# The tail of a hybrid attention block: weight parts made in pieces and parked in DRAM, sums on VectorE, products of two groups interleaved

## The chip, the core and the metric

The kernel runs on one core of a Trainium2 chip. The time is the device time of one launch in microseconds (us), the median of several runs. "The profile" is a page on one execution of the program, recorded on the chip; "the trace" is the record behind it, of which other views can be asked. TensorE is called PE there (its weight loads PEld), VectorE DVE, ScalarE ACT, GpSimd POOL and SyncE SP. SyncE computes nothing here: its queue issues the DMAs, in the order of the program.

## The reference

One encoder block over a sequence of 2048 rows of 1024 numbers. Only its end matters here:

```python
proj = h @ w_in                       # h = RMSNorm(x); q, k, v, ga, gb, mg are columns of proj
ya = banded_attention(...) * silu(ga)            # 2048 x 512
yb = sum_g(alpha_g * dilated_group_g(...)) * silu(gb)   # 2048 x 512
br_a, br_b = ya @ w_branch_a, yb @ w_branch_b    # 512 -> 1024 each
gates = sigmoid(mg + b_merge)                    # 2 x 2048 x 1024
merged = gates[0] * br_a + gates[1] * br_b
x = x + merged @ w_out                           # 1024 -> 1024
```

All is float32 and has to be accurate to about that, so each operand of a matmul is split into a high and a low float16 part, and a product is made of three matmuls: high by high, high by low, low by high.

## The kernel before

The kernel has a long part, in which the projections of 14 attention units and the attention itself are interleaved on TensorE (L1070 to L1108), and a **tail** (from L1113), which the change touches. The tail has four stages:

- **Plain gates** (`Std`, L1306): one 128-column chunk of the gate projection for 512 rows, 24 matmuls of 512 columns into one PSUM bank, 5.18 us by the program's plan. ScalarE takes a tanh from the bank, VectorE adds 1 (L1303), SP stores the tile to the DRAM array `mgd` (L1299). Chunk 1 comes first (eight groups), chunk 7 last (eight groups).
- **Gates in seven products** (`GateS`, L1354; `SiluS`, L1380): a 2x2 block product by Strassen's scheme in Winograd's form: seven block products in place of eight, paid for by sums of the operands and of the results. Gate chunks 2 to 6 and the three SiLU chunks 8 to 10 are done so, each in two groups (`SEQ`). A group is 84 matmuls of 512 columns, 18.13 us by plan. Its operands are sums of x (`s_build`, L1162: fourteen sums and differences and four casts for each of 4 chunks and 2 halves, parts on GpSimd and VectorE, into `SH`, `SL`) and sums of the weights (`w_sums` on GpSimd, `s_prep`). A SiLU group loads a tile of the attention output y from the DRAM array `ytd`, multiplies it by SiLU and stores it back.
- **Branches** (`Branch`, L1603): br_a and br_b for 2 x 128 rows, seven products of 24 matmuls of 128 columns. GpSimd multiplies the result by the gates and adds the two branches, and `m_build` makes the sums and float16 parts of `merged` for the last product.
- **Outputs** (`Out`, L1671): seven products of 12 matmuls of 512 columns; VectorE adds each finished bank to x (L1697), and SP stores the result.

The weights of branches and output need sums and float16 parts too: `wb_build` (L1469) makes those of the branches during the last gates and plain gates, `wo_build` (L1566) those of the output weights during the first branches, both from float32 loads, straight into the SBUF tiles that the matmuls read. `y_build` (L1521) does the same for y, its sums on GpSimd.

The seven products of a group use three banks. In `Seven` (L1319) the products have numbers 0 to 6 and the banks 0 to 2:

```python
PROD = (("A11", 0), ("S1", 2), ("A12", 1), ("S2", 0), ("S4", 2), ("S3", 0), ("A22", 0))
```

So product 3 goes on in the bank of product 0, 4 in that of 1, and 5 and 6 again in bank 0. Between two products of one bank its content must be read: by a copy on ScalarE (L1347), a sum on VectorE (L1351), or in `Out` the addition to x (L1697). The order on TensorE is written by hand in `run` (L1420): product 0 of a group, then product 6 of the group before, then products 1 to 5.

```python
def run(g):
    emit(g, 0)
    if pending:
        emit(pending.pop(), 6)
    if g.n == 7:
        for i in range(1, 6):
            emit(g, i)
        pending.append(g)
```

All other work is put on a heap by `at(t, f)` with a planned time t, and `emit` issues what is due between two matmuls. The planned times set only the order of the instructions in each engine's queue; each engine then runs its queue in order and waits for what is missing. Result tiles are `t2` tiles (nine buffers of 128 x 512), raw and summed operands of gates `t3` tiles (eight).

Of the kernel before, what the change touches and what calls it, by code (L numbers as in the profile page):

```python
# [74 lines left out]
Y_MAX = (0.02, 0.445, 0.485)  # L75
X_SQ = (5.098, 1.401, 9.651, 2.051)
# [15 lines left out]
def block_kernel(tc, x, w_units, w_gate, w_mrg, w_out, w_bra, w_brf, gain, qkg, sink, bias_a, bias_b, b_merge, out):  # L92
# [1028 lines left out]
    tp = tl.enter_context(tc.tile_pool(name="tp", bufs=9, reuse_waits="tile"))  # L1121
# [7 lines left out]
    t3p = t3s.enter_context(tc.tile_pool(name="t3p", bufs=8, reuse_waits="tile"))  # L1129
# [3 lines left out]

    def t3():
        return t3p.tile([128, 512], F32, name="t3")

# [25 lines left out]
    def s_build(q, ch):  # L1162
# [10 lines left out]
        def new(k, a, b, op, E=V):  # L1173
            r[k] = t3()
            E.tensor_tensor(r[k][:], a, b, op)  # L1175
# [7 lines left out]
        def lo(j, k):  # L1183
            V.tensor_tensor(SL[q][:, j, ch, :], r[k][:], SH[q][:, j, ch, :], OP.subtract)  # L1184

        return ((0, lambda: new(0, l21, l22, OP.add, G)), (.1, lambda: new(5, l11, l21, OP.subtract, G)),
                (.2, lambda: new(3, h11, h21, OP.subtract, G)),
                (1, lambda: new(1, h21, h22, OP.add)),
                (3, lambda: more(1, r[0][:], OP.add)), (3.1, lambda: hi(0, 1)),
                (4, lambda: more(3, r[5][:], OP.add)), (4.1, lambda: hi(2, 3)),  # L1190
                (5, lambda: new(2, r[1][:], h11, OP.subtract)), (6, lambda: more(2, l11, OP.subtract)),
                (6.1, lambda: hi(1, 2)), (7, lambda: lo(0, 1)), (8, lambda: lo(2, 3)),
                (9, lambda: new(4, h12, r[2][:], OP.subtract)), (10, lambda: more(4, l12, OP.add)),
                (10.1, lambda: hi(3, 4)), (11, lambda: lo(1, 2)), (12, lambda: lo(3, 4)))
# [11 lines left out]
    def w_sums(b11, b12, b21, b22, like, tile):  # L1206

        t = [like(tile()) for _ in range(4)]

        def f1():  # L1210
            G.tensor_tensor(t[0], b12, b11, OP.subtract)

        def f2():
            G.tensor_tensor(t[1], b22, b12, OP.subtract)

        def f3():
            G.tensor_tensor(t[2], t[1], b11, OP.add)

        def f4():
            G.tensor_tensor(t[3], b21, t[2], OP.subtract)  # L1220

        return (b11, t[0], b21, t[2], b22, t[1], t[3]), (f1, f2, f3, f4)
# [4 lines left out]
    def w_ready(dc, b):  # L1227
# [3 lines left out]
        def square(i):  # L1231
            raw = wtiles[u][0]
            if i == 0:
                wtiles[u].append(sm.tile([128, 4], F32, name="wsq"))
            A.activation(t3()[:].rearrange("p (c n) -> p c n", c=2), raw[:, 2 * i:2 * i + 2, :256], AF.Square,
                         accum_out=wtiles[u][1][:, i:i + 1])
# [14 lines left out]
        at(b + 20.5, total)  # L1251
        at(b + 21, power)

    def s_prep(dc, b):
# [4 lines left out]
        def split():  # L1259
# [5 lines left out]
                                lambda t: t[:].rearrange("p (c n) -> p c n", c=4), t3)  # L1265
# [14 lines left out]
        for k, i in enumerate((0, 2, 4, 1, 5, 3, 6)):  # L1280
            at(b + .3 + .9 * k, hi, i)
            at(b + 1.1 + .9 * k, lo, i)
# [18 lines left out]
    def m_gate(dst, src, dc, k, im, t0, d):  # L1301
        at(now[0] + d, lambda: A.activation(dst, src, AF.Tanh, bias=bmh[:, 8 * k + dc:8 * k + dc + 1], scale=im[:]))
        at(now[0] + d + .8, lambda: V.tensor_scalar(dst, dst, 1.0, None, OP.add))  # L1303
# [15 lines left out]
    class Seven:  # L1319
# [25 lines left out]
        def copy(self, j, b):  # L1345
            self.r[j] = t2()
            at(now[0] + .2, lambda: A.activation(self.r[j][:], b[:], AF.Copy))  # L1347

        def sum(self, j, b):
            r = self.r[j]  # L1350
            at(now[0] + .2, lambda: V.tensor_tensor(r[:], b[:], r[:], OP.add))  # L1351
            self.out(j, r, 1.0)
# [27 lines left out]
    class SiluS(GateS):  # L1380
        def __init__(self, g, q):
            super().__init__(8 + g, q)
            self.c0 = 2 + 2 * g

        def silu(self, src, n, t0, d, own):
            im = wtiles[NU + self.dc, "im"]
            c, k = self.c0 + n, 4 * (self.c0 + n) + t0 // 512
            y, th = t2(), t2()
            g = src if own else th
            nc.sync.dma_start(out=y[:], in_=ytd[c, :, t0:t0 + 512])  # L1390
# [28 lines left out]

    def run(g):  # L1420
        emit(g, 0)
        if pending:
            emit(pending.pop(), 6)
        if g.n == 7:
            for i in range(1, 6):
                emit(g, i)
            pending.append(g)

    def flush():
        if pending:  # L1430
            emit(pending.pop(), 6)

    for q in range(2):
        for ch in range(4):
            for d, f in s_build(q, ch):
                at(7.5 * (4 * q + ch) + 12.0 * q + .61 * d, f)
    SEQ = ((2, 0), (3, 0), (2, 1), (3, 1), (8, 0), (8, 1), (9, 0), (9, 1), (10, 0), (10, 1), (4, 0), (4, 1),
           (5, 0), (6, 0), (5, 1), (6, 1))
    first = 41.5
    ready, b = .5, 0.0  # L1440
    for dc, free in ((2, 0.0), (3, 0.0), (8, 3), (9, 4), (10, 6), (4, 8), (5, 10), (6, 12)):
        b = max(first + 18.13 * free + .3 if free else 0.0, ready + 22.0)
        w_ready(dc, ready)
        s_prep(dc, b)
        ready = b + 8.0
    w_ready(7, max(ready, first + 18.13 * 13))
    std_prep(7, first + 18.13 * 15 + .5)
    ym = []
    at(first + 18.13 * 11, lambda: ym.append(y_scale()))
    at(first + 18.13 * 11 + 1.5, lambda: ym.append(norm_sum(ym[0][:], 1)))  # L1450
    at(first + 18.13 * 11 + 2.0, lambda: y_scales(ym[1]))
    wb_raw, WB = {}, [None, None]

    def wb_tiles(k):
        WB[k] = [big(x) for x in "hl"]
# [4 lines left out]
    def wb_load(j):  # L1460
        k, p = divmod(j, 4)
# [355 lines left out]
```

## Time and profile before

| what | value |
| --- | --- |
| median of 3 runs | 2053.19 us (2051.21 to 2054.68) |
| the profiled execution's own time | 2057.84 us |
| its span, first to last instruction | 2056.1 us |
| mean granted TensorE clock | 0.972 |
| busy: PE, PEld | 1923.4, 1462.6 us |
| busy: DVE, ACT, POOL | 1488.5, 1209.0, 821.0 us |
| DMA | 279.79 MB, mean 136 GB/s |

A busy time is the sum over the whole span; it mixes the long part, where TensorE hardly ever pauses, with the tail, where it does. The granted clock is the share of full speed that TensorE was allowed to run at. In a row of groups of instructions a line is one of the kernel file, `fps<-bigh,wh` names what is written and read, and `x256` counts instructions; durations are in ns. A matmul's recorded length is longer than the distance to the next one, since matmuls are pipelined: its pace is read from the starts.

### The profile page before, as it was taken

To read this page: it belongs to the slowest core of one execution; us is meant where nothing else is said; L and a number is where in the kernel's file an instruction comes from. 1 tells how busy PE (TensorE), PEld (TensorE's weight loads), DVE (VectorE), ACT (ScalarE), POOL (GpSimd) and SP (SyncE) were. 2 spreads that over 40 slices of the span, in tenths; PEclk is the share of its full clock that TensorE was granted. 3 is DMA by queue.
4 is the path that set the end of the run, shared out by engine and by line. 5 is a ranking of instruction groups with operands and counts; after the bars stand their busy time and mean duration, and the time that the engine had idled before them with its cause. 6 is when DMAs were issued, how large, how long until landed. Compare 5 with 4: busy or idle time off the path is not lost.

```text
span 2056.1 us, 50959 instructions
## 1 busy us (share of the span) xinstructions
PE 1923.4 (94%) x19278; PEld 1462.6 (71%) x19278; DVE 1488.5 (72%) x3578; ACT 1209.0 (59%) x2917; POOL 821.0 (40%) x1599
## 2 busy tenths in 40 slices
PE   4999999999999999999999999789999985898998
PEld 3568977889998999999998964334444454665664
DVE  5679879867886688668876687965763669666664
ACT  8578768877777677667766663444444544323331
POOL 1033334343543355334533344422121248566552
PEclk9999999999999999999999999899999986999999
DMA  6259998977986698778985682113443253533341
GB/s 233 82 97 197 161 178 145 199 158 137 182 168 133 130 184 154 149 148 135 171 157 105 121 165 80 56 67 122 138 135 119 98 164 98 149 103 119 114 136 55
DMA packets 595446, 279.79 MB, mean 136 GB/s; under 512 B 456704, under 2 KB 550016, under 8 KB 594176
## 3 DMA queue, kind: packets, MB, share of 16 engines
q1 hardware_dynamic: 595200, 276.55, 60.1%
q8 instruction: 150, 2.46, 0.5%
q14 instruction: 96, 0.79, 0.1%
HBM read 115.75 MB, written 50.59 MB: 81 GB/s over the span
## 4 chain that ended last, share of the span: by engine, by line
PE 74%; DVE 12%; DMA 5%; issue 3%; ACT 3%; POOL 2%; SPq 1%; DVEq 0%; POOLq 0%; ACTq 0%
PE pj L625 40%; PE fps L1367 11%; PE fps L1616 6%; PE fps L1690 5%; PE s L775 4%; PE pv L824 4%; PE pj L287 3%; DMA pt<-p 2%; DVE mf L1663 2%; DVE t L1178 1%; DVE bigl L1184 1%; DVE t L1175 1%; PE fps L287 1%; DMA kq<-spl 1%; DVE wl L1275 1%
## 5 line engine op out<-in xcount | busy, mean ns | idle before, releaser
L625 PE MATMUL pj<-wl,XH 128*128 128x128 f16 (+2 forms) x2816 | 716.0, 268 | 0.0
L625 PE MATMUL pj<-wh,XL 128*128 128x128 f16 (+2 forms) x2816 | 712.3, 269 | 0.0
L625 PE MATMUL pj<-wh,XH 128*128 128x128 f16 (+2 forms) x2816 | 709.5, 268 | 0.0
L625 PEld LDWEIGHTS <-XH 128*128 128x128 f16 x5632 | 575.4, 112 | 54.6
L625 PEld LDWEIGHTS <-XL 128*128 128x128 f16 x2816 | 316.0, 112 | 24.1
L790 DVE CUSTOM_DVE_ANT_0 pr<-s,b,ubuf 128x256 f32<-128x256 f32 (+3 forms) x512 | 219.2, 465 | 70.2 <-PE s L775 66.9
L807 DVE SCALAR_TENSOR_TENSOR p<-pr,p 128x512 f16<-128x512 f32 (+2 forms) x256 | 194.9, 761 | 66.0 <-ACT p L803 62.0
L692 POOL TENSOR_TENSOR rw<-rw,g 128x128 f32<-128x128 f32 (+1 forms) x224 | 136.2, 628 | 210.9 <-DVE rw L685 191.4
L1616 PE MATMUL fps<-y,bigh 128*128 128x128 f16 x1792 | 166.3, 228 | 35.4 <-ACT t L1347 24.2
L707 POOL COPY spl<-spl 128x256 f16<-128x256 f16 (+1 forms) x224 | 87.8, 421 | 258.7 <-DVE spl L702 258.7
L1367 PEld LDWEIGHTS <-wh 128*128 128x128 f16 x896 | 89.3, 100 | 135.7 <-issue 36.0
L643 ACT ACTIVATE rw<-pj 128x256 f32<-128x256 f32 (+1 forms) x224 | 87.4, 390 | 167.1 <-PE pj L625 166.6
L1616 PEld LDWEIGHTS <-bigh 128*128 128x128 f16 x1792 | 147.7, 103 | 42.1 <-issue 38.1
L1690 PE MATMUL fps<-WOh,mf 128*128 128x512 f16 x448 | 147.1, 401 | 25.5 <-DVE xr L1697 25.5
L803 ACT ACTIVATE p<-pr 128x512 f16<-128x512 f32 (+2 forms) x256 | 157.7, 616 | 15.5 <-DMA pt<-p 10.9
L1616 PE MATMUL fps<-y,bigl 128*128 128x128 f16 x896 | 163.6, 228 | 0.0
L775 PE MATMUL s<-kq 128*128 128x128 f16 (+1 forms) x1856 | 148.4, 218 | 5.8 <-DMA kq<-spl 4.9
L775 PEld LDWEIGHTS <-kq 128*128 128x128 f16 x2016 | 131.0, 98 | 22.2 <-issue 6.7
L1690 PEld LDWEIGHTS <-mf 128*128 128x128 f16 x672 | 67.6, 102 | 110.3 <-issue 43.3
L1347 ACT ACTIVATE t<-fps 128x512 f32<-128x512 f32 x96 | 56.7, 591 | 144.4 <-PE fps L1616 111.2
L824 PE MATMUL pv<-vt,pt 128*128 128x65 f16 (+1 forms) x2784 | 131.6, 193 | 8.9 <-DMA pt<-p 8.9
L824 PEld LDWEIGHTS <-pt 128*128 128x128 f16 x3024 | 119.5, 97 | 24.6 <-DMA pt<-p 11.4
(245 smaller groups left out, 4162.1 us busy)
## 6 DMA issues: line engine op xcount, KB each, us to landing
wraw<-in_w_units_dram SPq DMA_DIRECT2D x56, 384.0 KB, 4.7
g<-mgd SPq DMA_DIRECT2D x64, 256.0 KB, 5.5
mgd<-t SPq DMA_DIRECT2D x56, 256.0 KB, 2.1
wraw<-in_w_mrg_dram SPq DMA_DIRECT2D x44, 256.0 KB, 4.3
zd<-z SPq DMA_DIRECT2D x128, 66.0 KB, 1.9
zz<-zd SPq DMA_DIRECT2D x64, 132.0 KB, 3.5
xt<-in_x_dram SPq DMA_DIRECT2D x16, 512.0 KB, 9.8
ytd<-yo SPq DMA_DIRECT2D x32, 256.0 KB, 3.4
```

The lines of the kernel that those rows point to most:

```text
L625: out.append(lambda lhs=lhs, rhs=rhs, ch=ch, a=a, b=b, k=k: T.matmul(ps[:, a:b], lhsT=lhs[:, ch, :], rhs=rhs[:, ch, a:b], start=(k == 0), ...
L643: A.activation(self.rw[:, n * i:n * i + n], self.ps[i][:, :n], AF.Copy)
L692: G.tensor_tensor(q[:, i, :un.nq, :], q[:, i, :un.nq, :], g, OP.mult)
L707: G.tensor_copy(sp[:, i, nh:, :, :], sp[:, i, nq:nh, ::-1, :])
L775: T.matmul(self.sv[j][:, o:o + k1 - k0], lhsT=q[:, h, :], rhs=kt[:, un.nq + kh + v * un.nk, k0:k1], start=(v == 0), stop=(v == 1))
L790: V.tensor_tensor_reduce(out=self.pv[:, j, self.p0:self.p0 + W], in0=self.sv[j], in1=un.bias[:, self.h0 + j, self.b0:self.b0 + W], scale=I ...
L803: A.activation(self.sp[:, :128 * n], self.pr, AF.Copy, scale=PSC)
L807: V.scalar_tensor_tensor(self.sp[:, 128 * n:], self.pr, PSC, self.sp[:, :128 * n], OP.mult, OP.subtract)
L824: T.matmul(self.po[:, j, :w], lhsT=p[:, n * j + s, :], rhs=un.v[key][:, vh, c0:c0 + w], start=(k == 0 and s == 0), stop=(k == 2 and s == n ...
L1367: out.append(lambda w=w, lo=lo, ch=ch, k=k: T.matmul(ps[:], lhsT=w[:, i, ch, :], rhs=xform(f, lo, ch, self.q), start=(fresh and k == 0), s ...
L1616: out.append(lambda p=p, c=c, wl=wl, yl=yl, n=n: T.matmul(ps[:, 128 * p:128 * p + 128], lhsT=w[wl][:, i, c, p, :], rhs=y[:, yl, c, :], sta ...
L1690: out.append(lambda p=p, ml=ml, wl=wl, k=k: T.matmul(ps[:], lhsT=m[:, ml, p, :], rhs=WO[wl][:, i, p, :], start=(fresh and k == 0), stop=(k ...
```

## The change

The number of matmuls hardly changes; what makes their operands and in which order they run does.

1. **Sums of x** (`s_build`): all fourteen on VectorE. Chunk 2 of the gates is done plainly, in eight `Std` groups behind those of chunk 1, and leaves `SEQ`, which begins with the SiLU chunk 8 and has 14 groups instead of 16.
2. **Weight sums** (`w_sums`): on VectorE instead of GpSimd, one of them in place.
3. **Gates**: the 1 is added by ScalarE (`AF.Identity` with a bias tile) instead of VectorE. SiLU scales its bank copies as they are made, which saves a factor later, and loads its y tile when the product starts.
4. **Pieces**: `wb_build` and `wo_build` go. Sixteen pieces of branch and output weights are made during the seven pairs of gate groups (four loads, four sums, seven high and seven low parts, four stores each), with the unused 256 pad columns of `XH` and `XL` as buffers, and parked in the DRAM arrays `wbd` and `wod`. `wb_load` and `wo_load` fetch them before use.
5. **Interleaving** (`run`): in branches and outputs, products 5 and 6 of a group run inside the next group. The gates keep the old order (`run_g`).
6. **y and merged**: the sums of `y_build` and `m_build` and the merge of the two branches are on VectorE; GpSimd keeps only the products with the gates. High and low parts have planned times of their own (`M_AT`).
7. Buffers: `t2` six and a new `r2` three, `t3` seven and `t4` three, gates of branches 16 instead of 13.

The diff, cut to its core:

```diff
-        def new(k, a, b, op, E=V):
+        def new(k, a, b, op):
             r[k] = t3()
-            E.tensor_tensor(r[k][:], a, b, op)
+            V.tensor_tensor(r[k][:], a, b, op)
...
-        t = [like(tile()) for _ in range(4)]
+        t = [like(tile()), b12] + [like(tile()) for _ in range(2)]
         def f1():
-            G.tensor_tensor(t[0], b12, b11, OP.subtract)
+            V.tensor_tensor(t[0], b12, b11, OP.subtract)
...
-        at(now[0] + d + .8, lambda: V.tensor_scalar(dst, dst, 1.0, None, OP.add))
+        at(now[0] + d + .8, lambda: A.activation(dst, dst, AF.Identity, bias=ones[:, 0:1]))
...
+        def mm(self, i):
+            if i in (0, 1, 3, 5):
+                n, h = ((0, 0), (1, 0), 0, (1, 1), 0, (0, 1))[i]
+                self.load(n, 512 * self.q + 1024 * h)
+            return super().mm(i)
...
     def run(g):
         emit(g, 0)
-        if pending:
-            emit(pending.pop(), 6)
-        if g.n == 7:
-            for i in range(1, 6):
-                emit(g, i)
-            pending.append(g)
+        if g.n == 1:
+            late()
+            return
+        emit(g, 1)
+        late()
+        emit(g, 2)
+        emit(g, 3)
+        late()
+        emit(g, 4)
+        pending.extend(((g, 5), (g, 6)))
...
-    SEQ = ((2, 0), (3, 0), (2, 1), (3, 1), (8, 0), (8, 1), (9, 0), (9, 1), (10, 0), (10, 1), (4, 0), (4, 1),
-           (5, 0), (6, 0), (5, 1), (6, 1))
-    first = 41.5
+    SEQ = ((8, 0), (8, 1), (3, 0), (3, 1), (9, 0), (9, 1), (4, 0), (4, 1), (10, 0), (10, 1),
+           (5, 0), (5, 1), (6, 0), (6, 1))
+    GR = 18.13
+    first = 16 * 5.18
...
+    wbd = dr.tile([2, 2, 128, 7168], F16, name="wbd")
+    wod = dr.tile([128, 7, 2, 4, 512], F16, name="wod")
+    def piece(j, m, b):
...
+        def store(x, a, e):
+            o = 512 * c + 256 * m
+            d = (wbd[k, x].rearrange("p (i o) -> p i o", i=7)[:, a:e, o:o + 256] if j < 4
+                 else wod[:, a:e, x, j - 4, 256 * m:256 * m + 256])
+            nc.sync.dma_start(out=d, in_=(XH, XL)[x][:, a:e, S:SE])
+        def hi(i):
+            A.activation(place(0, i), r[0][0][i], AF.Copy, scale=sc[:])
+        def lo(i):
+            V.scalar_tensor_tensor(place(1, i), r[0][0][i], sc[:], place(0, i), OP.mult, OP.subtract)
+        at(b - 5.0, load)
+        at(b, sums)
+        for f in range(4):
+            at(b + .01 + .8 * f, lambda f=f: r[0][1][f]())
+        for i in range(7):
+            at(b + .9 + PS * i, hi, i)
+            at(b + 1.9 + PS * i, lo, i)
+        for a, e in ((0, 4), (4, 7)):
+            for x in range(2):
+                at(b + 1.9 + PS * (e - 1) + 1.0 + .1 * x, store, x, a, e)
+    for j in range(16):
+        piece(j // 2, j % 2, first + 2 * GR * P_AT[j][0] + P_AT[j][1])
...
-            G.tensor_tensor(s1, a21, a22, OP.add)
-            G.tensor_tensor(s2, s1, a11, OP.subtract)
...
+            o, a, b, op = r[2][n]
+            V.tensor_tensor(o, a, b, op)
...
-    WO = [rp.tile([128, 7, 4, 512], F16, name=f"WO{x}") for x in "hl"]
+    WO = rp.tile([128, 7, 2, 4, 512], F16, name="WO")
+    def wo_load(i):
+        nc.sync.dma_start(out=WO[:, i], in_=wod[:, i])
...
-            at(now[0] + t, lambda: G.tensor_tensor(a, a, b, OP.add))
+            at(now[0] + t, lambda: V.tensor_tensor(a, a, b, OP.add))
```

381 lines of the change are left out of this document (199 added, 182 removed).

## Prediction

> **What bounds the kernel now.** I read the page first: TensorE is busy almost everywhere up to about 1300 us, then in tenths that fall to 5. The change touches only the code behind the attention units, so I asked for the stretches of that tail, then who TensorE waited for, then the order of its matmuls.
>
> In the stretches, the columns are length, busy time of each engine, granted clock, DMA share and GB/s:
>
> ```profile
> 1256.00:1297.00 41.00, 41.00 (x193) 18.71 (x191) 38.97 (x53) 16.66 (x31) 18.27 (x12) 1.00 0.17 58
> 1297.00:1631.00 334.00, 309.00 (x1390) 138.64 (x1389) 217.48 (x378) 154.92 (x283) 69.36 (x56) 0.96 0.31 104
> 1631.00:1680.00 49.00, 49.00 (x395) 29.04 (x394) 31.88 (x53) 24.86 (x53) 22.15 (x26) 1.00 0.57 169
> 1680.00:1776.00 96.00, 53.45 (x516) 44.10 (x514) 79.81 (x80) 40.72 (x72) 74.79 (x55) 0.74 0.37 117
> 1776.00:1997.00 221.00, 204.17 (x2152) 142.26 (x2150) 139.83 (x194) 73.08 (x141) 128.12 (x107) 0.93 0.42 123
> 1997.00:2056.00 59.00, 53.79 (x477) 33.35 (x474) 25.72 (x35) 8.72 (x14) 17.57 (x13) 0.99 0.24 76
> ```
>
> The hole is at 1680 to 1776: TensorE 53 of 96 us at a clock of 0.74, VectorE 80, GpSimd 75. Whom TensorE waited for (total us, times, longest):
>
> ```profile
> PE fps L1690 <- DVE xr L1697: 25.5, 8, 7.1
> PE fps L1616 <- ACT t L1347: 24.2, 5, 7.9
> PE fps L1367 <- ACT t L1347: 19.7, 4, 7.4
> PE fps L1616 <- DVE t L1351: 11.3, 2, 7.3
> PE fps L1367 <- DVE t L1351: 5.2, 3, 3.9
> ```
>
> Together 85.9 us: a product that goes on in a bank waits until ScalarE (L1347) or VectorE (L1351, L1697) has read that bank. The pace of undisturbed matmuls is in the chain that ended last, the tail's first one in the order of time, and the matmuls of L287, L1367, L1616 and L1690, in that order, in the stretches by line:
>
> ```profile
> 1256.30 0.38 PE L287 MATMUL fps<-XH,wh 128*128 128x512 f16 x1
> ```
> ```profile
> 1782.75 16.08 PE fps L1616 x288
> 1798.83 2.59 PE fps L1690 x12
> ...
> 1996.79 16.08 PE fps L1616 x288
> ...
> 2049.65 2.76 PE fps L1690 x12
> ```
> ```profile
> 1256.00:2056.10 800.10, 83.80 (x387) 0.93 0.35 110
> 1256.00:2056.10 800.10, 303.45 (x1344) 0.93 0.35 110
> 1256.00:2056.10 800.10, 168.00 (x2688) 0.93 0.35 110
> 1256.00:2056.10 800.10, 162.42 (x672) 0.93 0.35 110
> ```
>
> A 128-column matmul takes 16.08/288 = 0.0558 us, a 512-column one 2.59/12 = 0.2158. The tail has 384 (three of the 387 are older) + 1344 + 672 = 2400 wide ones, 517.9 us, and 2688 narrow ones, 150.0: 668 us without a pause. It ran from 1256.3 to 2052.4, 796.1 us. So 128.1 us are lost, 85.9 in waits and 42 to a slow clock after waits:
>
> ```profile
> 1435.73 0.38 PE L1367 MATMUL fps<-bigh,wh 128*128 128x512 f16 x1 [3.25 <-ACT t L1347]
> ...
> 1437.33 0.63 PE L1367 MATMUL fps<-bigh,wh 128*128 128x512 f16 x1
> 1437.76 0.63 PE L1367 MATMUL fps<-bigl,wh 128*128 128x512 f16 x1
> ...
> 1498.59 0.38 PE L1367 MATMUL fps<-XH,wh 128*128 128x512 f16 x1 [1.10 <-DVE t L1351]
> ```
>
> After a wait of 3.25 us matmuls start 0.43 apart, some eight of them, which costs about 8 x 0.21 = 1.7 us more; after 1.10 us they keep 0.38 long. By stage: eight plain groups fill 8 x 24 x 0.2158 = 41.4 us with no loss, to 1297.7. Gates to 1631.4 take 333.7 for 295.2 of work, **loss 38.5**. Seven plain groups, 36.3, none. From 1667.7 to the mark 1782.75 lie 672 + 24 narrow and 84 wide, 57.0 us of work in 115.1, **loss 58.1**. The next five rounds last (1996.79 - 1782.75)/5 = 42.81 each for 84 wide and 336 narrow, 36.9: **loss 29.6**. The rest 2.0. VectorE is full (38.97 of 41 us) as the gates begin; along the second loss it shares the work with GpSimd (80 and 75 of 96).
>
> **The change part by part.** Durations, least/median/most ns:
>
> ```profile
> L1184 DVE TENSOR_TENSOR bigl<-t,bigh x32: 677/684/1800, 1262.8 to 1361.5; 128x512 f16<-128x512 f32 x32
> ```
> ```profile
> L1351 DVE TENSOR_TENSOR t<-fps,t x96: 673/691/693, 1320.9 to 2012.9; 128x512 f32<-128x512 f32 x96
> ```
> ```profile
> L1275 DVE SCALAR_TENSOR_TENSOR wl<-wraw,ubuf,wh x24: 736/746/1639, 1292.6 to 1558.0; 128x512 f16<-128x512 f32 x24
> ```
> ```profile
> L1545 DVE SCALAR_TENSOR_TENSOR y<-t,ubuf,y x64: 470/485/1489, 1656.5 to 1999.6; 128x256 f16<-128x256 f32 x64
> ```
> ```profile
> 1238.76 0.43 DVE L994 TENSOR_TENSOR ya<-ya,zz 128x256 f32<-128x256 f32 x1
> ```
> ```profile
> L1697 DVE SCALAR_TENSOR_TENSOR xr<-fps,ubuf,xr x56: 735/750/752, 1755.4 to 2052.4; 128x512 f32<-128x512 f32 x56
> ```
> ```profile
> L1658 DVE TENSOR_TENSOR t<-g x8: 678/1751/1756, 1732.1 to 2021.1; 128x512 f32<-128x512 f32 x8
> L1626 POOL TENSOR_TENSOR g<-g,t x48: 1265/1272/1712, 1672.5 to 2015.0; 128x512 f32<-128x512 f32 x48
> ```
> ```profile
> L1347 ACT ACTIVATE t<-fps x96: 572/597/597, 1312.6 to 2010.2; 128x512 f32<-128x512 f32 x96
> ```
> ```profile
> L1302 ACT ACTIVATE t<-t,bmh,ubuf x30: 800/813/816, 1321.6 to 1624.4; 128x512 f32<-128x512 f32 x30
> ```
> ```profile
> L1271 ACT ACTIVATE wh<-t,ubuf x32: 705/707/717, 1296.9 to 1560.8; 128x512 f16<-128x512 f32 x32
> ```
> ```profile
> L1485 ACT ACTIVATE bigh<-t,ubuf x44: 492/496/508, 1590.3 to 1660.2; 128x256 f16<-128x256 f32 x44
> ```
> ```profile
> L345 ACT ACT_TABLE_LOAD x1 | 1.3, 1283 | 0.0
> ```
>
> *TensorE.* Gate chunk 2 becomes eight plain groups: 2 x 84 wide matmuls go, 192 come, so +24 x 0.2158 = **+5.2 us**; work is now 673.2 us. This is paid on the path, and buys 41.4 us in which plain groups, which need only ScalarE, cover the sums of x.
>
> *Sums of x on VectorE.* A sum takes 0.684 with GpSimd silent, up to 1.8 beside it; before, three of fourteen were on GpSimd. Now 8 x 14 x 0.684 = 76.6 us in 82.9 us of plain groups. To the end of the first gate pair VectorE also has forms of chunk 2 (4 x 0.746), of two gate chunks (2 x (4 x 0.684 + 7 x 0.746) = 15.9), two SiLU groups of three sums, eight products and four maxima at about 0.72 each (21.8) and one piece (4 x 0.43 + 7 x 0.485 = 5.1): 122.4 against 82.9 + 36.3 = 119.2 of TensorE. It overflows by 3.2; with a slow spell of 1.7 I charge 4.9. The two later SiLU pairs hold 21.8 + 8.0 + 5.1 = 34.9 of 36.3 on VectorE, piece over forms in places: 3 each. That the y of SiLU is now fetched ahead takes a wait off VectorE.
>
> *Plain gate pairs.* The "+1" goes from VectorE to ScalarE. No row shows that form there; L1347 (0.597) and L1302 (0.813) bound it, and I take 0.70, since it has one pointer less than L1302. A pair on ScalarE: 2 x (3 x 0.597 + 4 x 0.813 + 4 x 0.70) = 15.7, forms 7 x 0.707 = 4.9, squares 4 x 0.6 (an estimate from L1347, of the same size), three pieces 21 x 0.496 = 10.4: 33.4 of 36.3. It fits; where copies queue behind forms I charge 0.8 in each of four pairs. **Gates: 4.9 + 6 + 3.2 = 14** (3 if everything fits, 35 if VectorE stays behind).
>
> *Pieces.* The 8 + 4 builds of branch and output weights leave the stretches from 1590 to 1776 and come back as 16 pieces under the gates; each issues four loads and four stores on SP's queue, 128 together, and 15 loads bring the parts back. One issue takes
>
> ```profile
> L1299 SPq DMA_DIRECT2D mgd<-t x56: 319/320/683, 1265.9 to 1680.6; - x56
> ```
>
> so 41 to 87 us of SP's time over 254 us of gates. The pieces read 8.4 MB and write 14.7 (58 GB/s), under gates that moved 104 GB/s at a share of 0.31: covered. A wait is added on ScalarE: a piece's high parts go into the pad columns of XH, and the first of them must find the store of the piece before landed, with the gates' bank copies queued behind it. By plan that store is issued 4.4 us earlier; I charge nothing, and the bound of 35 below leaves (35 - 14)/16 = 1.3 a piece for it. TensorE would wait behind those copies, so a late store would show as a longer wait of L1367 on L1347. The output weights return in the 45 us before their use beside some 6 MB of gates, y and x: 13.4 MB, at 169/0.57 = 296 GB/s just 45 us. Nearly no slack; bounds 0 and 15 us, I take 3, since the first is needed 35 us after its issue.
>
> *Two groups interleaved.* In branches and outputs (the gates keep their order) products 5 and 6 of a group now run inside the next one. Product 5 had one product (1.34 us) between itself and the copy that it waits for, now four; product 6 one, now two: 2.7 us for a sum of 0.69, in outputs 2.7 for 0.75. This removes the waits of 3.4 in each round, and with the builds gone those of 1680 to 1750. What is late next is VectorE.
>
> *VectorE in a round.* 8 from banks x 0.691 = 5.5, 7 outputs x 0.75 = 5.3, 7 low parts x 0.746 = 5.2, 14 of half size x 0.485 = 6.8, and, from GpSimd, 8 sums and merges x 0.684 = 5.5 and 8 half sums x 0.43 = 3.4: 31.7 us. GpSimd keeps 6 products of 1.27. Each can cost VectorE 1.751 - 0.684 = 1.07 where it meets an operation on two SBUF tensors; that is 0 to 6.4, and as such operations fill 20.9 of 36.9 us I take 57%, 3.6. So **35.3 of 36.9**, against
>
> ```profile
> 1783.00:1997.00 214.00, 197.17 (x2103) 138.41 (x2101) 135.07 (x186) 70.49 (x135) 126.94 (x105) 0.94 0.42 124
> ```
>
> 135.07/5 = 27.0 now. TensorE stays the bound, barely; I charge 1.2 per round, six rounds, **7** (0, or 13 if VectorE needs its 38.1 and 1 of gaps). The rule of the Trainium skill, "SBUF — State Buffer", section "SBUF: two separate sides", is that the port pair shared by VectorE and GpSimd is locked for a whole instruction, and that the loser waits it out; the trace agrees as far as a bank-fed sum never passes 0.693 while L1658 has 1.751. By it each meeting would cost up to 1.27, at most 39.3 per round, and a time of some 1968.
>
> First branches: 3 for DMA and 3 for buffers (t2 falls from 9 to 6 and 3), **6**, from 58.1. End: product 5 and 6 of the last branch are flushed with nothing between, **3**.
>
> **The sum.** 14 + 6 + 7 + 3 = 30, so the tail takes 703.2 instead of 796.1: -92.9 us. The profiled execution took 2057.84 us for a span of 2056.1, 4.65 above the median of 2053.19; I subtract from the median: **1960.3 us**. 0.2%, 4 us, is what a measurement can tell.
>
> **The rivals.** (a) *Nearly no stall*, 5 left: 1935. For it: the stretch 1631 to 1680 already runs plain groups and the first branch products with TensorE at 49.00 of 49.00, VectorE and ScalarE having room; against: VectorE at 35.3 of 36.9 in a round. (b) *VectorE becomes the bound*: gates 35, first branches 15, rounds 13, end 4, 67 in all: 1997. (c) *A table load on each side of the new "+1"*: 56 x 2 x 1.283 us. Plain groups absorb it, a gate group needs 7.8 + 10.3 + 8.9 = 27 of 18.1 us, eight of them 71 more: 2031. The Trainium skill, "ScalarE: Activation LUTs", section "Table sets: the hidden batching unit", has identity in every set, which would rule this out; no run here shows it yet. (d) *Slower: SP's queue in order.* A piece's loads stand in SP until the last piece gives up its buffers, and the gate stores stand behind them, with t2 buffers held. Such a hold is in the trace:
>
> ```profile
> SPq L1573 <- POOL t L1214: 15.5, 2, 10.5
> ```
>
> Six t2 buffers at five uses per group turn round in 22 us, about 8 of which a use needs; so a hold under 14 us costs nothing. At 20 us each, 16 pieces stall 6 + 1.7: 123 us, 2083. Break-even is 92.9/16 = 5.8 us per piece. By plan a hold is 3 us. (e) *The waits only move* to product 6, still one sum away: as before, 2053.
>
> **How the numbers follow.** Forecast 0.62, (a) 0.11, (b) 0.16, (c) 0.03, (d) 0.06, (e) 0.02. Faster is 0.92, same 0.02, slower 0.06. The range leaves out half of (a) and the tails of (c), (d), (e): 1938 to 1998.
>
> **What would show it.** Right: TensorE near 9 tenths from 1680 on at full clock, rounds of 37 to 38.5 us, VectorE near 35 us in each, GpSimd under 8, few waits left, the longest in SiLU pairs. Wrong: waits of L1616 or L1690 on VectorE in every round (b), table loads between L1302 and the "+1" (c), waits of ScalarE's copies on stores (d), waits of 3 us at product 6 (e), or branch products waiting for loads of parked weights, which would put my DMA term at fault.

## The result, and the profile after

The changed kernel takes **1949.65 us** (four runs, 1949.03 to 1953.81) where the kernel before, in the same comparison, takes 2053.93 (2051.21 to 2055.58). The ratio is 0.9498 with a 95% interval of 0.9481 to 0.9515. The forecast of 1960.3 us is a ratio of 1960.3 / 2053.19 = 0.9548: the direction and nine tenths of the gain are right, and the rest, some 10 us, is more than the interval allows. The profiled execution took 1953.81 us for a span of 1952.0.

The page of the kernel after: busy times, then the rows of TensorE and of its granted clock in 40 slices. The tail begins in slice 26:

```profile
PE 1890.2 (97%) x19302; PEld 1446.3 (74%) x19302; DVE 1483.1 (76%) x3777; ACT 1241.1 (64%) x2992; POOL 557.2 (29%) x1375
...
PE   4999999999999999999999999999999999999998
...
PEclk8999999999999999999999999999999999999999
```

The hole is gone. GpSimd has 557 us where it had 821. The stretches of the tail (length, busy time of PE, PEld, DVE, ACT and POOL, granted clock, DMA share, GB/s):

```profile
1256.00:1340.00 84.00, 84.00 (x393) 38.47 (x392) 78.00 (x136) 48.65 (x85) 0.00 (x0) 1.00 0.23 79
1340.00:1594.00 254.00, 244.84 (x1141) 111.66 (x1139) 197.38 (x418) 167.62 (x330) 0.00 (x0) 1.00 0.62 189
1594.00:1636.00 42.00, 42.00 (x196) 19.03 (x195) 19.02 (x44) 24.60 (x47) 0.00 (x0) 1.00 0.90 316
1636.00:1710.00 74.00, 70.42 (x895) 55.29 (x894) 54.09 (x87) 31.48 (x59) 17.76 (x12) 1.00 0.76 246
1710.00:1931.00 221.00, 220.22 (x2445) 158.39 (x2444) 175.62 (x300) 79.07 (x150) 51.84 (x36) 1.00 0.45 133
```

The granted clock is 1.00 in each, where it was 0.74 at its lowest. The waits that are left (total us, times, longest), L1359 being the bank copy that was L1347, and L1370 and L1757 the reads that were L1351 and L1697:

```profile
PE fps L1385 <- DVE r L1418: 4.1, 5, 1.2
PE fps L1385 <- ACT t L1359: 4.1, 2, 2.5
PE fps L1678 <- DVE r L1370: 2.8, 3, 1.6
PE fps L1750 <- DVE xr L1757: 2.4, 2, 1.6
PE fps L1385 <- DVE r L1370: 1.0, 1, 1.0
```

That is 14.4 us for 85.9 before, and none is longer than 2.5. The tail's first matmul, and the chain that ended last, give its stages:

```profile
1256.91 0.38 PE L294 MATMUL fps<-XH,wh 128*128 128x512 f16 x1
```
```profile
1608.34 2.59 PE fps L1385 x12
1610.93 36.26 PE fps L294 x168
1647.19 5.37 PE fps L1678 x96
...
1712.25 10.72 PE fps L1678 x192
...
1749.14 10.72 PE fps L1678 x192
...
1859.81 10.72 PE fps L1678 x192
...
1945.56 2.77 PE fps L1750 x12
```

The pace is the same: 36.26/168 = 0.2158 us for a wide matmul, 10.72/192 = 0.0558 for a narrow one. So the losses can be worked out as they were for the kernel before:

| stage | work | lasted | lost | before | forecast |
| --- | --- | --- | --- | --- | --- |
| 16 plain groups, 1256.91 to 1339.8 | 82.9 | 82.9 | 0 | 0 | 0 |
| gates, to 1610.93 | 259.0 | 271.1 | **12.1** | 38.5 | 14 |
| plain groups, to 1647.19 | 36.26 | 36.26 | 0 | 0 | 0 |
| first branches, to 1712.25 | 61.0 | 65.1 | **4.1** | 58.1 | 6 |
| four rounds, to 1859.81 | 147.56 | 147.56 | **0** | 29.6 (five) | 7 (six) |
| rest, to 1948.33 | 86.5 | 88.5 | **2.0** | 2.0 | 3 |
| all | 673.2 | 691.4 | **18.2** | 128.1 | 30 |

Of the gates' 12.1 us, 9.2 are in the waits above (4.1, 4.1 and 1.0), and sixteen small matmuls (L179), which the count of work leaves out, are recorded with 2.3 more at most.

### The profile page after: what moved, and what is told of

The parts are those of the page before. It is cut to its first block, busy times and chain, and to the rows that moved or that the text cites. A ratio compares the mean times of both kernels' runs of the same rounds, so it can differ in the third digit from the quotient of the medians.

```text
span 1952.0 us, 51050 instructions
## 1 busy us (share of the span) xinstructions
PE 1890.2 (97%) x19302; PEld 1446.3 (74%) x19302; DVE 1483.1 (76%) x3777; ACT 1241.1 (64%) x2992; POOL 557.2 (29%) x1375
## 4 chain that ended last, share of the span: by engine, by line
PE 80%; DVE 8%; DMA 6%; ACT 3%; issue 2%; SPq 1%; POOL 0%; DVEq 0%; POOLq 0%; ACTq 0%
PE pj L632 41%; PE fps L1385 9%; PE fps L1750 7%; PE fps L1678 6%; PE fps L294 5%; PE s L782 5%; PE pv L831 4%; PE pj L294 3%; DMA pt<-p 2%; DMA kq<-spl 2%; DVE wl L1287 1%; PE pt L895 1%; ACT jk L428 1%; DVE XL L1555 0%; DVE pr L797 0%
## 5 line engine op out<-in xcount | busy, mean ns | idle before, releaser
L1688 POOL TENSOR_TENSOR g<-g,t 128x512 f32<-128x512 f32 x32 | 48.6, 1519 | 550.2 <-DMA g<-mgd 405.4
L714 POOL COPY spl<-spl 128x256 f16<-128x256 f16 (+1 forms) x224 | 88.5, 425 | 257.6 <-DVE spl L709 257.6
L1678 PE MATMUL fps<-y,bigh 128*128 128x128 f16 x1792 | 153.7, 219 | 2.8 <-DVE r L1370 2.8
L1750 PE MATMUL fps<-WO,mf 128*128 128x512 f16 x672 | 150.3, 379 | 2.4 <-DVE xr L1757 2.4
L1385 PEld LDWEIGHTS <-wh 128*128 128x128 f16 x784 | 76.8, 98 | 101.9 <-issue 11.7
L1678 PE MATMUL fps<-y,bigl 128*128 128x128 f16 x896 | 151.8, 219 | 0.0
L1678 PEld LDWEIGHTS <-bigh 128*128 128x128 f16 x1792 | 139.2, 98 | 10.5 <-issue 3.2
L831 PEld LDWEIGHTS <-pt 128*128 128x128 f16 x3024 | 119.9, 98 | 23.9 <-DMA pt<-p 10.7
L1750 PEld LDWEIGHTS <-mf 128*128 128x128 f16 x672 | 64.5, 98 | 74.7 <-issue 2.8
```

Source lines behind the costliest of these rows:

```text
L714: G.tensor_copy(sp[:, i, nh:, :, :], sp[:, i, nq:nh, ::-1, :])
L831: T.matmul(self.po[:, j, :w], lhsT=p[:, n * j + s, :], rhs=un.v[key][:, vh, c0:c0 + w], start=(k == 0 and s == 0), stop=(k == 2 and s == n ...
L1385: out.append(lambda w=w, lo=lo, ch=ch, k=k: T.matmul(ps[:], lhsT=w[:, i, ch, :], rhs=xform(f, lo, ch, self.q), start=(fresh and k == 0), s ...
L1678: out.append(lambda p=p, c=c, wl=wl, yl=yl, n=n: T.matmul(ps[:, 128 * p:128 * p + 128], lhsT=w[wl][:, i, c, p, :], rhs=y[:, yl, c, :], sta ...
L1750: out.append(lambda p=p, ml=ml, wl=wl, k=k: T.matmul(ps[:], lhsT=m[:, ml, p, :], rhs=WO[:, i, wl, p, :], start=(fresh and k == 0), stop=(k ...
```

## The experiments

All twelve differ from one of the two kernels in a few lines. A difference in us is the difference of ratios times 2054, against the 0.9498 of the kernel after unless something else is said. Where two traces are compared, a mark is measured from the tail's first matmul, since the tail itself begins at different times: at 1256.91 us in the profiled execution of the kernel after, at 1250.4 to 1254.9 in those of its variants, by work that no edit touches.

**The old order on TensorE** (u_order). Branches and outputs run as the gates do:

```diff
-        run(Branch(s, 0))
+        run_g(Branch(s, 0))
...
-        run(outs[s])
+        run_g(outs[s])
```

> The changed kernel with the old order of products in branches and outputs (product 6 alone runs inside the next group). If the distance between a bank's read and the product that goes on in that bank made the waits of the rounds, they come back although VectorE is relieved: 4 to 6 us in each of six rounds and 5 to 10 in the first branches, 1979 to 1996 us. If the waits came from the queues of VectorE and GpSimd and the order only moved with them, under 1960 us and rounds below 38.5 us.

Measured: 1954.97 us, ratio 0.9512 (0.9496 to 0.9528), 2.9 us more, with intervals that overlap. My theory was that the distance between the products takes away the waits of the rounds; it **failed here**. The chain of this kernel shows its rounds:

```profile
1709.96 16.08 PE fps L1678 x288
...
1858.46 16.08 PE fps L1678 x288
```

(1858.46 - 1709.96)/4 = 37.13 us for a round, 0.24 over the work in it. So with the old order, too, the waits of 3.4 us do not come back in the rounds. The first branches do show one wait of 5.5 us, where the kernel after has 1.6:

```profile
PE fps L1678 <- DVE r L1370: 6.3, 2, 5.5
```

The trace of before, read again at one such wait, says why. VectorE in order of time, then the matmul that waited:

```profile
1897.66 0.47 DVE L1545 SCALAR_TENSOR_TENSOR y<-bigh,ubuf,y 128x256 f16<-128x256 f32 x1
1898.05 1.21 DVE L1663 SCALAR_TENSOR_TENSOR mf<-t,ubuf,mf 128x512 f16<-128x512 f32 x1
1899.18 0.94 DVE L1545 SCALAR_TENSOR_TENSOR y<-bigh,ubuf,y 128x256 f16<-128x256 f32 x1
1900.05 0.74 DVE L1663 SCALAR_TENSOR_TENSOR mf<-t,ubuf,mf 128x512 f16<-128x512 f32 x1
1900.71 0.47 DVE L1545 SCALAR_TENSOR_TENSOR y<-bigl,ubuf,y 128x256 f16<-128x256 f32 x1
1901.10 0.74 DVE L1697 SCALAR_TENSOR_TENSOR xr<-fps,ubuf,xr 128x512 f32<-128x512 f32 x1
```
```profile
1901.90 0.58 PE L1690 MATMUL fps<-WOh,mf 128*128 128x512 f16 x1 [3.36 <-DVE xr L1697]
```

TensorE stopped at 1901.90 - 3.36 = 1898.54, behind product 4 of the outputs. Product 5 goes on in the bank of product 3, which was finished one product of 2.59 us earlier, at about 1895.95. The reader of that bank, L1697, started only at 1901.10, 5.1 us later, because the reader of another bank (at 1897.00) and the five operations on y and merged that are shown stood ahead of it in VectorE's queue, two of them stretched (1.21 for 0.74, 0.94 for 0.47). The wait was the queue of VectorE, and more distance is one of two ways to survive it.

**The new order alone** (b_order). The kernel before gets `run`, `run_g` and `late`, the buffers and the planned times that belong to them; sums and weight builds stay. At its two flushes a product begins before its bank is read; that wait is left out there:

```diff
+        emit(g, 1)
+        late()
+        emit(g, 2)
+        emit(g, 3)
+        late()
+        emit(g, 4)
+        pending.extend(((g, 5), (g, 6)))
```

> The kernel before with the new order of products in branches and outputs alone, and the buffers and planned times that it needs (r2, g, mf, xr, sums of merged in the gate tiles); sums stay on GpSimd, weights are built where they were. If order makes the waits of the rounds: rounds of 37 to 39 us instead of 42.8 and little change in the first branches, which the builds hold up: 2010 to 2028 us. If GpSimd and VectorE make them: rounds above 41 and 2040 us or more.

Measured: 2025.13 us, ratio 0.9854 (0.9835 to 0.9872), 30.0 us less than before. Its chain and the longest of its waits:

```profile
1778.09 10.72 PE fps L1636 x192
...
1929.59 10.72 PE fps L1636 x192
```
```profile
PE fps L1636 <- DVE r L1354: 31.1, 4, 13.5
```

Rounds of (1929.59 - 1778.09)/4 = 37.88 us, for 42.81: the order alone is enough as well. The first branches still wait, up to 13.5 us.

**No build of the output weights** (b_nowo). In the kernel before ScalarE copies branch weights into `WO` in place of loads, sums and parts; that work is left out:

```diff
-        at(b + .01 + 1.2 * f, lambda f=f: r[0][1][f]())
-        for n, i in enumerate((0, 2, 4, 1, 5, 3, 6)):
-            at(b + .4 + .8 * n, hi, i)
-            at(b + 1.2 + .8 * n, lo, i)
+        for x in range(2):
+            at(b + 9.5 + .1 * x, lambda x=x: A.activation(WO[x][:, :, p, :], WB[0][x][:, :3584].rearrange(
+                "p (i n) -> p i n", i=7), AF.Copy))
```

> The kernel before, in which the output weights are not built: their loads, sums and low parts are left out, and ScalarE copies parts of the branch weights into their place (so the outputs are not the reference's). If the builds on VectorE and GpSimd hold up the first branches: the loss of 58 us there falls by 25 to 45, the rounds stay at 42.8: 2009 to 2029 us. If the order of products makes that loss too: 2040 us or more.

Measured: 2028.30 us, ratio 0.9866 (0.985 to 0.9883), 27.5 us less than before. Its chain reaches the mark of the first round earlier:

```profile
1753.61 16.08 PE fps L1611 x288
```

Measured from the tail's first matmul (1254.53 here, 1256.30 before) that is 499.1 us for 526.5, so 27.4 us less: nearly half of the 58.1 lost in the first branches. What the loads are worth in this, and what the sums and parts, isn't separated. The rounds keep their 42 to 43.2.

**Both together** (b_nowo_order, the two edits above; the same work is left out).

> Both of the last two edits on the kernel before; the output weights are left out here too. If the two causes are separate their gains add: about 30 for the order and 45 to 55 for the builds, 1967 to 1982 us, with the loss of 38 us in the gates still there. If one hides the other, it is near the better of the two alone, above 2000 us.

Measured: 1998.02 us, ratio 0.972 (0.9699 to 0.974), 57.5 us less than before. I had expected 1967 to 1982: the size was missed, since I put the builds at 45 to 55 where they are worth 27.5 (the order was put at 30). The two add up (30.0 + 27.5 = 57.5): builds and order act at different places. Its rounds last (1901.94 - 1750.46)/4 = 37.87 us, and the first begins 496.4 us after the tail's first matmul (1750.46 - 1254.09), for 455.3 in the changed kernel (1712.25 - 1256.91). So 41 of the 45.6 us that still lie between the two are lost earlier, in gates and first branches.

**Sums of y and merged, and the merge of the branches, back on GpSimd** (u_ysum):

```diff
-            V.tensor_tensor(o, a, b, op)
+            G.tensor_tensor(o, a, b, op)
...
-            at(now[0] + t, lambda: V.tensor_tensor(a, a, b, OP.add))
+            at(now[0] + t, lambda: G.tensor_tensor(a, a, b, OP.add))
```

> The changed kernel, with the sums of y and of merged and the merge of the branches back on GpSimd; the new order of products stays. If either measure alone keeps TensorE fed in the rounds (the order gives the bank reads time, the relief makes them prompt), rounds stay under 38.5 us: 1950 to 1960 us. If the move of the sums is what counts, the alternation of VectorE and GpSimd comes back and rounds go to 41 or more: above 1972 us.

Measured: 1959.52 us, ratio 0.9542 (0.9527 to 0.9557), 9.0 us more. Its chain has rounds of 1748.80 - 1710.90 = 37.90 us, the length that the new order alone gave:

```profile
1710.90 10.72 PE fps L1678 x192
...
1748.80 10.72 PE fps L1678 x192
```

**Both undone** (u_ysum_order, the edits of u_order and u_ysum). If the two measures stand in for each other, undoing both must cost more than 2.9 + 9.0.

> The changed kernel with those sums back on GpSimd and the old order of products in branches and outputs as well. If the two measures replace each other, undoing both brings back what undoing one did not: waits of 2 to 4 us behind VectorE in each round, rounds of 40 to 43 us, 1972 to 1995 us. If the two are independent and small, about 1955 plus what the sums alone cost, under 1965 us.

Measured: 1978.97 us, ratio 0.9638 (0.9616 to 0.9659), **28.8 us** more. The chain and the wait that came back:

```profile
1713.22 16.36 PE fps L1678 x288
...
1878.80 16.08 PE fps L1678 x288
```
```profile
PE fps L1750 <- DVE xr L1757: 22.0, 8, 3.7
```

Rounds of (1878.80 - 1713.22)/4 = 41.4 us, near the 42.81 of before, and the wait on the read of the output bank is there again, eight times, up to 3.7 us. One of them ends at 1792.89 after 2.92 us; the reader started 2.1 us after TensorE had stopped, behind other operations of VectorE's queue, as in the kernel before, and VectorE's low parts of y take 0.657 us there on average for 0.477 in the kernel after. This settles the rounds: the waits need both a VectorE queue that GpSimd's operations lengthen and products that stand close; each half of the change alone takes away nearly all of them.

**Three sums of x per chunk back on GpSimd** (u_xsum), as before the change:

```diff
-            V.tensor_tensor(r[k][:], a, b, op)
+            E.tensor_tensor(r[k][:], a, b, op)
...
+        return ((0, lambda: new(0, l21, l22, OP.add, G)), (1, lambda: new(1, h21, h22, OP.add)),
...
+                (3, lambda: new(5, l11, l21, OP.subtract, G)), (4, lambda: new(3, h11, h21, OP.subtract, G)),
```

> The changed kernel with three of the fourteen sums of x of each chunk back on GpSimd, as before the change; sixteen plain groups still run ahead of the gates. If the lock between VectorE and GpSimd made the loss of the first gates, VectorE falls behind again and the first pair waits: 5 to 20 us more, 1955 to 1970 us. If the 41 us more of plain groups ahead are what removed it, within 3 us of the changed kernel, 1947 to 1953 us.

Measured: 1957.88 us, ratio 0.9534 (0.9518 to 0.955), 7.4 us more. The waits on the bank copies grow from 4.1 to 9.3 us, and the longest, at the first pair of gate groups, from 2.5 to 7.7:

```profile
PE fps L1385 <- ACT t L1359: 9.3, 2, 7.7
```

By the traces the first round begins 8.8 us later (1716.71 - 1252.54 = 464.2 us after the tail's first matmul, for 455.3). The longer waits are 5.2 of it, and some thirteen matmuls behind the wait of 7.7, which start 0.43 us apart, about 13 x 0.21 = 2.8.

**The "+1" back on VectorE** (u_plus1):

```diff
-        at(now[0] + d + .8, lambda: A.activation(dst, dst, AF.Identity, bias=ones[:, 0:1]))
+        at(now[0] + d + .8, lambda: V.tensor_scalar(dst, dst, 1.0, None, OP.add))
```

> The changed kernel with the 1 of the gates added by VectorE again. VectorE gets 56 operations of 0.43 us in gates and plain groups, ScalarE loses 56 of 0.71. If VectorE is what the gates wait for, their loss of 12 us grows by 2 to 6: 1952 to 1956 us. If ScalarE is (copies behind forms and pieces), it falls by 1 to 4: 1946 to 1949 us.

Measured: 1960.49 us, ratio 0.9548 (0.9532 to 0.9565), 10.3 us more: the direction is right, the size larger than the 2 to 6 that I gave it. The trace has 8.8 us more ahead of the first round (1718.79 - 1254.60 = 464.2). Most of the loss is at the same place:

```profile
PE fps L1385 <- ACT t L1359: 8.6, 2, 7.0
```

Two quite different reliefs of VectorE end in the same wait, that of the first gate pair on a copy of ScalarE.

**More work on VectorE in the rounds** (dve7, dve14). Seven or fourteen operations without effect per output group, to find how near VectorE is to the bound:

```diff
+            for k in range(1):      # range(2) in dve14
+                at(now[0] + .9 + .01 * k, lambda: V.tensor_tensor(t[:], t[:], t[:], OP.max))
```

> The changed kernel with seven operations added on VectorE in each output group, one behind each finished tile: the maximum of the 128 x 512 tile with itself, about 0.6 us of queue time each, 4.3 per round. By my sum of before the result VectorE had 35.3 of 36.9 us in a round; with 4.3 more it would be the bound, rounds of 39 or more, 12 us more in all: above 1960 us. By the trace of the changed kernel it has 29.8, so 34.1 still fits: rounds stay near 36.9, 1949 to 1954 us.

> The changed kernel with fourteen such operations per output group, 8.6 us per round. With 29.8 measured VectorE would have 38.4 us in a round, over TensorE's 36.9: rounds of 38 to 40, 8 to 20 us more, 1957 to 1970 us. By the sum of 35.3 it would be 43.9: 42 us more, 1992. If VectorE's queue doesn't bound at all, within 4 us of the changed kernel.

Measured: dve7 1966.04 us, ratio 0.9568 (0.9551 to 0.9586), 14.4 us more; dve14 1990.63 us, ratio 0.9691 (0.9672 to 0.971), 39.6 more. Two views of dve14 and the wait that grows in dve7:

```profile
1717.00:1888.21 171.21, 154.76 (x1683) 109.85 (x1682) 158.49 (x265) 56.16 (x108) 34.56 (x24) 0.96 0.42 124
```
```profile
PE fps L1750 <- DVE xr L1757: 25.6, 7, 5.7
```
```profile
PE fps L1750 <- DVE xr L1757: 11.9, 7, 3.9
```

In dve14 a round lasts 171.21/4 = 42.80 us, and VectorE is busy for 158.49/4 = 39.6 of it. The kernel after has, over its four rounds:

```profile
1712.25:1859.81 147.56, 147.56 (x1684) 107.92 (x1681) 119.23 (x209) 55.74 (x108) 34.70 (x25) 1.00 0.49 145
```

119.23/4 = 29.8 of 36.89. By that busy time fourteen operations of (39.6 - 29.8)/14 = 0.70 us would find 7.1 us of room, and seven (4.9 us) would cost nothing. They do cost. When VectorE is the bound it still idles 42.80 - 39.6 = 3.2 us a round, waiting in order for inputs, so its queue needs 29.8 + 3.2 = 33.0 us; by the growth from dve7 to dve14, (39.6 - 14.4)/42 = 0.60 for each operation in six rounds, the seven of dve7 (4.2 a round) cost 2.4, so 1.8 was room and 36.9 - 1.8 = 35.1 the need. That 0.60 is less than the recorded 0.70 because VectorE's operations overlap: two sums recorded with 0.69 and 0.68 start 0.60 apart (at 1339.93 and 1340.53 in the kernel after). The rounds of the two traces, less the added operations at 0.60 us, give much the same: 42.80 - 8.4 = 34.4, and for dve7, whose rounds last 38.95 us, 38.95 - 4.2 = 34.8. **33 to 35 of 36.9**, and no more is shown. Both times came near what I had worked out from my 35.3 (above 1960, and 1992), not from the 29.8 of the trace (1949 to 1954, 1957 to 1970).

**The pieces' arithmetic left out** (nopiece): sums, high and low parts of the 16 pieces are not made, their loads and stores stay.

```diff
-        at(b, sums)
-        for f in range(4):
-            at(b + .01 + .8 * f, lambda f=f: r[0][1][f]())
-        for i in range(7):
-            at(b + .9 + PS * i, hi, i)
-            at(b + 1.9 + PS * i, lo, i)
```

> The changed kernel with the pieces' arithmetic left out: sums, high and low parts of the sixteen pieces (so the outputs are not the reference's); their loads, their stores (of what the pad columns hold) and the loads of the parked parts stay. If the pieces' work on ScalarE and VectorE makes a good part of the 12 us lost in the gates, 4 to 9 us less: 1941 to 1946 us. If the gates wait for the SiLU and form work alone, within 2 us of the changed kernel.

Measured: 1946.37 us, ratio 0.9472 (0.9456 to 0.9489): 5.3 us less by the ratios, 3.3 by the medians, and the intervals just overlap. The traces agree with the larger figure: the last matmul of the gates' seven products starts 348.2 us after the tail's first one (1603.11 - 1254.91), for 353.6 in the kernel after (1610.55 - 1256.91). So the pieces' arithmetic costs some 5 of the gates' 12.1 us; what their loads and stores cost is not in it.

**The output weights fetched twice** (wo_twice), 7.3 MB more in a stretch that has no DMA time left. In the kernel after SP issues these loads from 1653.65 to 1687.1 us, and that stretch has a DMA share of 0.98 at 328 GB/s (the stretch to 1636 with 0.90 holds the loads of the branch weights):

```profile
1653.60:1690.00 36.40, 34.40 (x546) 31.32 (x543) 34.71 (x50) 15.60 (x30) 14.29 (x10) 1.00 0.98 328
```

```diff
-        nc.sync.dma_start(out=WO[:, i], in_=wod[:, i])
+        for _ in range(2):
+            nc.sync.dma_start(out=WO[:, i], in_=wod[:, i])
```

> The changed kernel with each part of the parked output weights loaded twice, 7.3 MB more ahead of the first outputs. By my sum (13.4 MB in 45 us at 296 GB/s, no slack) that is 25 us more of DMA time on the way of the first outputs and gates: 10 to 25 us more, 1960 to 1975 us. By the 316 GB/s at a share of 0.90 that the changed kernel's trace shows, about 20 us of DMA in a stretch with some 10 idle: 5 to 12 more. If the loads run well ahead of their use, under 2 us.

Measured: 1984.40 us, ratio 0.9659 (0.9642 to 0.9676), 33 us more, where I had expected 10 to 25. Waits of TensorE, then one of VectorE and one of SP's queue:

```profile
PE fps L1751 <- DVE xr L1758: 15.1, 3, 13.1
PE fps L1679 <- ACT y L1625: 12.0, 1, 12.0
```
```profile
DVE xr L1758 <- DMA xr<-in_x_dram: 6.8, 1, 6.8
SPq L1657 <- DMA WO<-wod: 45.9, 7, 7.5
```

The weights are not what TensorE waits for in these rows: the tiles of y, x and the gates, asked for behind them, come late. The last row says why, and it isn't the bytes alone. Each second load goes into the tile of the first, so SP's queue stands still until the first has landed: seven times, 45.9 us in all, with everything behind it in the queue. From 1650 to 1702 us the DMA share is 0.81, below the 0.88 of the kernel after, though there is more to move. So this run shows what a held queue costs there; what 7.3 MB more would cost without the hold is not shown. Rounds behind that stretch keep their 36.89 us.

## Why the prediction was right, and which term was off

**TensorE.** 24 more matmuls, as counted (19302 for 19278), at the same pace; plain groups without a pause. The 5.2 us were paid; what the 41 us of cover that they bought are worth was not tried by itself. The 42 us that I put to a slow clock were a remainder, lost time less waits; the kernel after has such a remainder, too, 18.2 - 14.4 = 3.8 us, at a granted clock of 1.00, so a part of it need not be the clock.

**Sums of x.** 4.9 us were charged for the first gate pair, and its waits are 2.46 and 1.17, 3.6. The way there was another than I gave. I had VectorE's bank reads arrive late; it was ScalarE's. ScalarE, the waiting matmul, and VectorE in order of time:

```profile
1343.91 0.63 ACT L1194 ACTIVATE bigh<-t 128x512 f16<-128x512 f32 x1 [1.30 <-DVE t L1191]
1344.44 0.76 ACT L1314 ACTIVATE t<-fps,bmh,ubuf 128x512 f32<-128x512 f32 x1
...
1349.73 0.67 ACT L1359 ACTIVATE t<-fps,ubuf 128x512 f32<-128x512 f32 x1
```
```profile
1350.45 0.38 PE L1385 MATMUL fps<-bigh,wh 128*128 128x512 f16 x1 [2.46 <-ACT t L1359]
```
```profile
1343.79 1.47 DVE L1197 TENSOR_TENSOR bigl<-t,bigh 128x512 f16<-128x512 f32 x2
```

VectorE is still on the sums of x at 1343.79 + 1.47 = 1345.3, 5.5 us after the plain groups ended. The last cast of x on ScalarE waits for one of them, and the remaining tanhs, "+1" and squares stand in ScalarE's queue behind that cast, the bank copy behind them. u_xsum and u_plus1 make VectorE later still, by different work (its last sum of x ends 93.6 and 94.4 us after the tail's first matmul, for 88.4), and it is this copy that is later each time (7.7 and 7.0): that supports the reading.

**The "+1" on ScalarE.** Rows of the kernel after:

```profile
L1315 ACT ACTIVATE t<-t,ones x48: 704/712/724, 1265.5 to 1648.0; 128x512 f32<-128x512 f32 x48
```

0.712 us where 0.70 was taken, at the even length of an instruction without a table load: rival (c) is out. By the Trainium skill, "ScalarE: Activation LUTs", section "Table sets: the hidden batching unit", identity is in every set; the trace agrees with these 48 instructions of 704 to 724 ns, and with eight more on other tiles of 705 to 722. That the move off VectorE is worth 9 to 10 us was in no term of mine.

**Pieces.** Covered, as costed: gates lost 12.1 for 14 charged, nopiece puts the pieces' arithmetic at 3 to 5 of it, and rival (d) is out: TensorE's waits in the gates come to 9.2 us, none over 2.5, and a piece's loads (L1536) held SP's queue for 2.5 us at the longest. One wait that I had charged with nothing did come, ScalarE's on the store of the piece before, of 5.1 us before 1607.97; no wait of TensorE on ScalarE follows it. The "nearly no slack" of the loads is right: a DMA share of 0.98, at 328 GB/s for the 296 of the sum. In the kernel itself the loads were in time; the first branches lost 4.1 for 6 charged.

**Two groups interleaved.** Here the reason failed while the number held. The prediction said of the distance from one product to four: "This removes the waits of 3.4 in each round". By b_order it does; by u_order the relief of VectorE's queue does as well, and only when both are undone do 28.8 us come back. I counted the distance as the cause and the sums' move from GpSimd as a cost (5.5 + 3.4 us on VectorE); the runs show this move as a second, sufficient cure. Rival (e), the waits move to product 6, is out: the longest of L1678 and L1750 is 1.6 us.

**VectorE in a round: the mis-sized term.** I had 35.3 of 36.9 us, and charged 1.2 us in each of six rounds, **7** in all. The four measured rounds last 36.89, and the loss is **0.0**. The need was nearly right: dve7 and dve14 put it at 33 to 35. The charge was wrong: below the bound nothing was lost, not even a little, with two to four us to spare. Of the signs that I named, VectorE near 35 us (29.8 busy) and GpSimd under 8 (34.70/4 = 8.7) did not come, and rounds were shorter than 37. The rest of the error comes from the gates and first branches (2 each) and the end (1): 30 forecast, 18.2 measured. These 11.8 us are the error, less 0.6 by which the tail began later and 0.5 by which the two profiled executions stand differently above their medians (4.65 and 4.16): 10.7.

That 35.3 came near the need is luck: its parts were off in both directions. I had added recorded lengths, which overlap: in the four rounds they add up to 134.1 us, 33.5 a round, where VectorE is busy for 29.8. Groups of VectorE in 1710 to 1931 of the kernel after (busy us, mean ns):

```profile
L1715 DVE TENSOR_TENSOR g<-g 128x512 f32<-128x512 f32 x24 | 16.4, 685 | 0.2
L1723 DVE SCALAR_TENSOR_TENSOR mf<-g,ubuf,mf 128x512 f16<-128x512 f32 x47 | 44.5, 949 | 5.5 <-ACT mf L1719 5.3
```

The sums of merged stay at 0.685, unhurt; the low parts take 0.949 for 0.746. So of the 3.6 a round that I gave to meetings with GpSimd, 7 x 0.2 = 1.4 us are seen in that group. (The rule of the Trainium skill, "SBUF — State Buffer", section "SBUF: two separate sides", that the loser of the shared port waits a whole instruction out, fits the stretched low parts, whose median is 0.746 and whose longest is 1.774; the 39.3 us a round that it allowed at most did not come, with rounds of 36.89.) On the other side stands waiting in order, which I had at nothing: 5.3 us of idle ahead of `mf` on ScalarE's high parts in this one group.

**The rivals.** (a), nearly no stall, is where the rounds went, not the gates: 18.2 us lost, between its 5 and the forecast's 30. (b) did not happen, but is near: the seven operations of dve7 in each round bring it, with rounds of 38.95 us and the waits on L1757. Left open: what chunk 2 as plain groups is worth (undoing it takes 41 us of cover with it) and what parking the pieces is worth as a whole in the kernel after; neither was tried. None of the runs that do the full work is faster than the kernel after.

## What to carry to other kernels

When a matmul waits for the read of its bank, look at what stands ahead of the reader in its engine's queue before asking for more distance: distance and a shorter queue each removed these waits, and their gains don't add (2.9 and 9.0 us undone singly, 28.8 together). An engine that is busy 81% of a round can be out of room, since it also waits in order; adding a few operations without effect measures the room that a busy time can't show. An engine just below the bound cost nothing here: charge a stall only where an engine's need, its waiting in order included, passes the round. And an experiment that adds a load tests the queue as well as the bytes: look at what the added load itself waits for.

## What the runs showed of the hardware that was not expected

- Waits of up to 2.46 us left the granted clock at 1.00 in every stretch of the kernel after. The kernel before showed matmuls at 0.43 after one wait of 3.25, and in dve7 twelve wide matmuls behind a wait of 3.93 took 5.28 us for 2.75. The length of the wait alone doesn't decide it: the four rounds of dve14, at a clock of 0.96, have four waits of 3.6 us, and the twelve matmuls behind them took 4.34, 2.75, 4.43 and 5.28.
- Of GpSimd's 48 products 32 have a median of 1.451 us, with VectorE's sums beside them, for 1.272 before (the other 16 have 1.298):

```profile
L1688 POOL TENSOR_TENSOR g<-g,t x32: 1266/1451/1727, 1652.1 to 1908.3; 128x512 f32<-128x512 f32 x32
```

- With only six operations of GpSimd a round VectorE's low parts still take 0.949 us on average for 0.746, by a few that reach 1.774, while the sums of merged between them keep 0.685. Which operations are lengthened goes by where they stand: in u_order it is the merges of the branches as well (0.947 for 0.684).
- DMA ran at 328 GB/s at a share of 0.98 with no wait of TensorE on the weights. Second loads into the same tiles there, 7.3 MB whose transfer alone would take 7300/328 = 22 us, held SP's queue for 45.9 us and cost 33.
